# A two-layer decoder trunk: the second half of the features in two parts before each norm, and the last norm on VectorE alone

## The chip, the core and the metric

The kernel runs as one program on one core of a Trainium2 chip. The metric is the device time of one execution in microseconds (us). A core has TensorE (PE in the views; its weight loads are PEld), VectorE (DVE), ScalarE (ACT), GpSimd (POOL) and SyncE (SP), each with its own queue of instructions in program order, and 16 DMA engines. A row that ends in a letter q after the engine's name, as SPq, is an instruction that issues a DMA.

## The reference

The input is 256 rows of 1024 features in float32. There are two layers, and each is

```python
h = layer_norm(ALPHA * h + mix, ln1_g, ln1_b)     # mix: three attention branches, gates, w_out
ffn = (silu(conv3(h @ w_gate) + b) * (h @ w_val)) @ w_down      # D_FF = 2816
h = layer_norm(ALPHA * h + ffn, ln2_g, ln2_b)
# layer_norm(x): (x - mean) * rsqrt(var + 1e-5) * g + b, over the 1024 features of a row
```

The output is h after the second layer, 256 x 1024 float32.

## The kernel before

**Tiles.** The rows are two blocks of 128, `tb` 0 and 1; a block lies on the 128 partitions. `h[tb][q]` is a block's half of the features, 512 columns. Every product is made of three fp32r matmuls (`mm3`: high by high, low by high, high by low); one `mm3` per step k of the contraction is called a unit here. Weights stream from HBM in order of use through `raw` tiles (queue SP) and are split by ScalarE and VectorE into the pairs `hl`.

**The norms.** Four times a norm follows a product: the output projection (first and third norm) and the down projection (second and fourth). Just before each, the last eight units' weights are held ready, and the loop runs `tb`, then `PIECES` (nh, first column, end column), then k: four units for each piece, and then `ln_half`, which on VectorE adds the PSUM bank to ALPHA times h (SCALAR_TENSOR_TENSOR, h<-h,acc) and takes the statistics (BATCH_NORM_STATS2, bst<-h). When both halves of a block are done, `ln_stats` aggregates (mv<-bst), adds epsilon, and lets GpSimd raise to the power -0.5 (rs<-mv,mhalf). `ln_apply` then does, for each half, h<-h,mv,lng (subtract the mean, times g) and h<-h,rs,lnb (times rs, plus b). `ln_tail` transposes each half on TensorE (att<-ident,h, four 128x128 per half) and splits the result into `hTh` (ScalarE) and `hTl` (VectorE, hTl<-att,hTh), the next product's stationary operands. That product takes block 0 first (eight units of 512 columns, k 0 to 3 from the first half of the features, 4 to 7 from the second), then block 1.

**The order.** The program is written out by a planner in Python. Work around the main product lies in generators; `T.tick()`, called after every unit, lets each go on to its next `yield`, and then lets at most one more weight tile be split. A generator yields until its input is due by the planner's own clocks: an instruction starts at its engine's clock or when its inputs are due, and its result is due 150 ns after its end. TensorE takes work only when its clock is 300 ns past that.

```python
rate = {F32: 4, R32: 1, BF16: 1}[args[1].dtype] / 2.4
return n * rate + {F32: 5, R32: 13.3, BF16: 3}[args[1].dtype]   # PE; a transpose is 110
return 60 + n * (0.53 if op in ("tensor_copy", "tensor_scalar") else 1.05)   # DVE
return 75 + 0.85 * n                                            # ACT
return 630 if n <= 16 else 100 + 2.2 * n                        # POOL
while any(clocks.done.get(x.name, 0) > clocks.now(eng) - MARGIN.get(eng, 0) for x in aps):
    yield                                                       # MARGIN = {"PE": 300.0}
```

These clocks order the program; they are no part of its time on the chip. While `W.hold` is set (through a norm) weight tiles are split only when fewer than three are in reserve.

**The last norm.** Behind the fourth norm there is no product. Block 0's is a generator, `last_norm0`: ScalarE normalizes both halves, GpSimd multiplies and adds for the first half, VectorE for the second, which it takes up before block 1's second half. Block 1's is `last_norm1`, on VectorE. Each half is stored as it is done: 128 rows of 2 KB, through the queues of SP and ScalarE.

Of the kernel before, what the change touches and what calls it, by code (L numbers as in the profile page):

```python
# [14 lines left out]
AF = mybir.ActivationFunctionType  # L15
ALU = mybir.AluOpType
AX = mybir.AxisListType

P = 128
# [3 lines left out]
DEPTH = 2  # L23
# [9 lines left out]
           biw=2884, cq=2892, ck=3404, cv=3916)  # L33
NG1 = 332

PIECES = ((0, 0, 512), (1, 0, 512))
MASKED = -1.0e38
PICKED = -3.0e38
PICK_T = -2.0e38
# [248 lines left out]
def tile_hybrid(ctx: ExitStack, tc: tile.TileContext, a: dict, out: bass.AP):  # L288
    nc = tc.nc
    clocks = Clocks()  # L290
    ve, sc = Engine(nc.vector, "DVE", clocks), Engine(nc.scalar, "ACT", clocks)
    pe, gp = Engine(nc.tensor, "PE", clocks), Engine(nc.gpsimd, "POOL", clocks)
# [15 lines left out]
    T = Tasks(clocks, W)  # L308
# [3 lines left out]
    def nm(s):  # L312
        uid[0] += 1
        return f"{s}_{uid[0]}"
# [19 lines left out]
    def small(shape, n="sm"):  # L334
        return ss.tile(shape, F32, name=nm(n), tag="sm")
# [7 lines left out]
    def ready(eng, *aps):  # L343
        while any(clocks.done.get(x.name, 0) > clocks.now(eng) - MARGIN.get(eng, 0) for x in aps):
            yield
# [4 lines left out]
    def mm3(o, lh, ll, rh, rl, start, stop):  # L350
        mm(o, lh, rh, start, False)
        mm(o, ll, rh, False, False)
        mm(o, lh, rl, False, stop)


    h = [[hp.tile([P, 512], F32, name=f"h{t}{q}") for q in range(2)] for t in range(2)]
# [3 lines left out]
    lng = hp.tile([P, D], F32, name="lng0", tag="lng")  # L360
    lnb = hp.tile([P, D], F32, name="lnb0", tag="lnb")
# [106 lines left out]
    def ln_half(tb, q, st, bank=None, cols=(0, 512), slot=None):  # L468

        hs = h[tb][q][:, cols[0]:cols[1]]  # L470
        if bank is not None:
            ve.scalar_tensor_tensor(hs, hs, ALPHA, bank[:, cols[0]:cols[1]], ALU.mult, ALU.add)
        ve.bn_stats(st[:, q if slot is None else slot, :], hs)

    def ln_stats(st):

        mv = small([P, 2], "mv")
        ve.bn_aggr(mv, st)
        ve.tensor_scalar(mv[:, 1:2], mv[:, 1:2], LN_EPS, None, ALU.add)
        rs = small([P, 1], "rs")  # L480
        gp.tensor_tensor(rs, mv[:, 1:2], mhalf[:, :1], ALU.pow)
        return mv[:, 0:1], rs
# [5 lines left out]
            ve.scalar_tensor_tensor(y, y, mu, gq, ALU.subtract, ALU.mult)  # L488
            ve.scalar_tensor_tensor(y, y, rs, bq, ALU.mult, ALU.add)

    def store(tb, q):
        (nc.sync, sc)[q].dma_start(out[0, tb * P:(tb + 1) * P, 512 * q:512 * q + 512], h[tb][q])

    def last_norm1(st, g, b):
        mu, rs = ln_stats(st)
        for q in range(2):
            ve.scalar_tensor_tensor(h[1][q], h[1][q], mu, g[:, 512 * q:512 * q + 512], ALU.subtract, ALU.mult)
        for q in range(2):
            ve.scalar_tensor_tensor(h[1][q], h[1][q], rs, b[:, 512 * q:512 * q + 512], ALU.mult, ALU.add)
            store(1, q)  # L500

    def last_norm0(st, g, b, half_done):

        mu, rs = ln_stats(st)
        nmr = small([P, 1], "nmr")
        ve.scalar_tensor_tensor(nmr, mu, -1.0, rs, ALU.mult, ALU.mult)
        for q in range(2):
            sc.activation(h[0][q], h[0][q], AF.Identity, bias=nmr, scale=rs)
        gp.tensor_tensor(h[0][0], h[0][0], g[:, 0:512], ALU.mult)
        gp.tensor_tensor(h[0][0], h[0][0], b[:, 0:512], ALU.add)  # L510
        while not half_done:
            yield
        ve.tensor_tensor(h[0][1], h[0][1], g[:, 512:1024], ALU.mult)
        ve.tensor_tensor(h[0][1], h[0][1], b[:, 512:1024], ALU.add)
        store(0, 1)
        yield from ready("POOL", h[0][0])
        nc.sync.dma_start(out[0, 0:P, 0:512], h[0][0])

    def transpose4(dst, src, n=4):
        for i in range(n):  # L520
# [6 lines left out]
    def ln_tail(tb, st, hT, g, b, flag):  # L527

        ln_apply(tb, st, g, b)
        yield  # L530
        for q in range(2):
            yield from ready("PE", h[tb][q])
            bk = yield from att()
            transpose4(bk, h[tb][q])
            split_out(hT[0][:, 4 * q:4 * q + 4, tb * P:(tb + 1) * P],
                      hT[1][:, 4 * q:4 * q + 4, tb * P:(tb + 1) * P],
                      bk.rearrange("p (k t) -> p k t", k=4))
            att_free()
        flag.add(tb)
        W.hold = len(flag) < 2  # L540
# [60 lines left out]
    def layer(l, hT, hflag):  # L601
# [384 lines left out]
        lng = hp.tile([P, D], F32, name=nm("lng"), tag="lng")  # L986
        lnb = hp.tile([P, D], F32, name=nm("lnb"), tag="lnb")
# [4 lines left out]
        def gate():  # L992
            bk = unit_x(lhs, KD, 512)
            g = t4([P, 2, 512], n="gs")
            for tb in range(2):
                sc.activation(g[:, tb, :], bk[tb], AF.Sigmoid)
            return g
# [7 lines left out]
        for key in ("oB", "oA"):  # L1005
            for nh in range(2):
                g = gate()
# [46 lines left out]
        hT1, flag1 = new_hT(), set()  # L1054
        for tb in range(2):
            ts = slice(tb * P, (tb + 1) * P)
            st = small([P, 2, 6], "bst")
            for i, (nh, c0, c1) in enumerate(PIECES):
                for k in range(4):
                    w = ws[nh][k][:, :, c0:c1]  # L1060
                    mm3(ob[nh][tb][:, c0:c1], mT[1][:, 0, k, ts], mT[1][:, 1, k, ts], w[:, 0, :], w[:, 1, :],
                        False, k == 3)
                    if tb and c1 == 512:
                        W.free()
                    if True:
                        T.tick()
                ln_half(tb, nh, st, ob[nh][tb], (c0, c1), i)
            T.add(ln_tail(tb, st, hT1, lng, lnb, flag1))
# [29 lines left out]
        lng = hp.tile([P, D], F32, name=nm("lng"), tag="lng")  # L1098
        lnb = hp.tile([P, D], F32, name=nm("lnb"), tag="lnb")
# [61 lines left out]
        hT2, flag2 = new_hT(), set()  # L1161
        for tb in range(2):
            ts = slice(tb * P, (tb + 1) * P)
            st = small([P, 2, 6], "bst")
            for i, (nh, c0, c1) in enumerate(PIECES):
                for d in (NPAIR - 2, NPAIR - 1):
                    T.until(lambda: d in acts)
                    for f in range(2):
                        w = ws[d, f, nh][:, :, c0:c1]
                        mm3(dacc[nh][tb][:, c0:c1], acts[d][:, 0, f, ts], acts[d][:, 1, f, ts],  # L1170
                            w[:, 0, :], w[:, 1, :], False, d == NPAIR - 1 and f == 1)
                        if tb and c1 == 512:
                            W.free()
                        if True:
                            T.tick()
                ln_half(tb, nh, st, dacc[nh][tb], (c0, c1), i)
                if l == DEPTH - 1 and tb and nh == 0:
                    half_done.append(1)
                    T.tick()
            if l < DEPTH - 1:  # L1180
                T.add(ln_tail(tb, st, hT2, lng, lnb, flag2))
            elif tb == 0:
                half_done = []
                T.add(last_norm0(st, lng, lnb, half_done))
            else:
                last_norm1(st, lng, lnb)
        return hT2, flag2


# [29 lines left out]
    for l in range(DEPTH):  # L1219
        hT, hflag = layer(l, hT, hflag)  # L1220
        T.tick()
        while T.live:
            if l < DEPTH - 1 and len(hflag) < 2:
                break
            T.tick()
# [51 lines left out]
```

## Time and profile before

| | us |
|---|---|
| median of 3 runs (lowest, highest) | 935.33 (933.94, 935.53) |
| the profiled execution | 935.33 |
| its span, first to last instruction | 933.5 |
| TensorE busy | 905.1 (97%) |
| VectorE busy | 656.0 (70%) |
| ScalarE busy | 513.5 (55%) |
| GpSimd busy | 47.3 (5%) |

The time of an execution is some 1.8 us longer than its span. Nearly all instructions carry line 240, the line of the helper that records them, so the views are read by tile names: `h<-h,acc` is an instruction that writes h and reads h and acc. In a timeline each line gives the start in us, the busy time in us, the engine, the operation, the tiles, the shapes, how many instructions are merged, and in brackets how long the engine had been idle before and who ended that. PEclk is the clock granted to TensorE as a share of full speed.

### The profile page before, as it was taken

The numbers are of one execution on the slowest core, as the hardware profiler recorded it, in microseconds if no ns is written. First come the engines' busy times: TensorE is split into PE (matmuls) and PEld (weight loads), VectorE is DVE, ScalarE is ACT, GpSimd is POOL, SyncE is SP. The second block draws the span as 40 slices with busy tenths as digits, with TensorE's granted clock in tenths as the row PEclk, the third lists the DMA queues.
The fourth block names the chain that finished last, engine by engine and source line by source line (L and its number), as shares of the span: only waits on it lengthen the run. The fifth ranks groups of instructions, "written<-read, shape, count | busy, mean of one in ns | idle before, by whom it ended". The sixth has DMA issues, their size and how long they took to land.

```text
span 933.5 us, 14405 instructions
## 1 busy us (share of the span) xinstructions
PE 905.1 (97%) x5306; PEld 791.1 (85%) x5306; DVE 656.0 (70%) x1270; ACT 513.5 (55%) x1008; POOL 47.3 (5%) x62
## 2 busy tenths in 40 slices
PE   4999999999999999999999999999999999999995
PEld 2877897888888999999988789888888799999994
DVE  7788677567678766666788966865667886766755
ACT  4654666655536655655456455765554375655541
POOL 6000010001000000000010000100110100000001
PEclk9999999999999999999999999999999999999998
DMA  8843256656535766566345332846665286566601
GB/s 306 275 141 113 69 178 232 188 193 194 181 121 207 245 194 189 172 197 190 113 159 180 123 113 70 298 143 201 192 197 171 87 298 196 181 194 188 182 3 45
DMA packets 46536, 161.45 MB, mean 173 GB/s; under 512 B 5697, under 2 KB 6209, under 8 KB 46465
## 3 DMA queue, kind: packets, MB, share of 16 engines
q1 hardware_dynamic: 44208, 154.94, 51.5%
q0 software_dynamic: 1408, 4.98, 1.7%
q8 instruction: 41, 0.67, 0.3%
q10 hardware_dynamic: 848, 0.60, 0.2%
q14 instruction: 31, 0.25, 0.1%
HBM read 159.46 MB, written 1.05 MB: 172 GB/s over the span
## 4 chain that ended last, share of the span: by engine, by line
PE 70%; issue 21%; DVE 6%; DMA 1%; POOL 1%; ACT 0%; SPq 0%; ACTq 0%; DVEq 0%; POOLq 0%
PE acc L240 49%; PE att L240 21%; DVE h L240 2%; DVE s L240 1%; DMA raw<-in_w_dram 1%; POOL rs L240 1%; DVE hl L240 1%; DMA cst<-in_cst_dram 1%; DVE bst L240 1%; DVE mx L240 0%; DVE mv L240 0%; DVE hTl L240 0%; DVE t L240 0%; ACT h L240 0%; POOL hl L240 0%
## 5 line engine op out<-in xcount | busy, mean ns | idle before, releaser
L240 DVE TENSOR_TENSOR hl<-raw,hl 128x512 fp32r<-128x512 f32 (+1 forms) x581 | 389.5, 696 | 191.3 <-ACT hl L240 189.7
L240 ACT ACTIVATE hl<-raw 128x512 fp32r<-128x512 f32 (+1 forms) x584 | 347.8, 625 | 189.5 <-PE att L240 92.4
L240 PE MATMUL acc<-hl,hTh 128*128 128x512 f32 (+1 forms) x896 | 285.9, 392 | 4.1 <-DVE hl L240 2.0
L240 PE MATMUL att<-hTh,hl 128*128 128x256 f32 x1280 | 231.3, 283 | 0.0
L240 PEld LDWEIGHTS att<-hTh,hl 128*128 128x128 f32 x1280 | 200.8, 192 | 1.4
L240 PEld LDWEIGHTS acc<-hl,hTh 128*128 128x128 f32 x896 | 168.3, 189 | 39.5 <-DVE hl L240 2.7
L240 PE MATMUL att<-hTl,hl 128*128 128x256 f32 x640 | 181.1, 283 | 0.0
L240 PE MATMUL acc<-hl,hTl 128*128 128x512 f32 (+1 forms) x448 | 173.3, 387 | 1.8 <-DVE hTl L240 1.8
L240 PE MATMUL acc<-hl,act 128*128 128x512 f32 x528 | 123.4, 390 | 0.0
L240 PEld LDWEIGHTS att<-hTl,hl 128*128 128x128 f32 x640 | 122.8, 192 | 0.0
L240 PEld LDWEIGHTS acc<-hl,act 128*128 128x128 f32 x528 | 97.9, 188 | 19.5
L240 PEld LDWEIGHTS acc<-hl,hTl 128*128 128x128 f32 x448 | 85.0, 190 | 17.8 <-DVE hTl L240 2.7
L240 PE MATMUL acc<-hl,oT 128*128 128x512 f32 x288 | 68.0, 391 | 0.0
L240 PEld LDWEIGHTS acc<-hl,oT 128*128 128x128 f32 x288 | 53.8, 188 | 11.0
L240 DVE SCALAR_TENSOR_TENSOR cv<-att,convp,cv 128x255 f32<-128x255 f32 x88 | 40.4, 480 | 15.4 <-ACT cv L240 13.9
L240 PE MATMUL acc<-hTh,hl 128*128 128x256 f32 x256 | 47.7, 287 | 0.0
L240 PE MATMUL acc<-hl,mT 128*128 128x512 f32 x192 | 45.4, 392 | 0.0
L240 ACT ACTIVATE hTh<-att 128x512 fp32r<-128x512 f32 x16 | 9.6, 598 | 59.2 <-PE att L240 59.1
L240 PEld LDWEIGHTS acc<-hl,mT 128*128 128x128 f32 x192 | 35.6, 188 | 7.1
L240 PEld LDWEIGHTS acc<-hTh,hl 128*128 128x128 f32 x256 | 39.8, 191 | 2.0 <-issue 1.7
L240 PE MATMUL acc<-hTl,hl 128*128 128x256 f32 x128 | 36.2, 283 | 0.0
L240 POOL TENSOR_TENSOR rs<-mv,mhalf 128x1 f32<-128x1 f32 x10 | 9.1, 906 | 482.4 <-DVE mv L240 482.4
(160 smaller groups left out, 696.6 us busy)
## 6 DMA issues: line engine op xcount, KB each, us to landing
raw<-in_w_dram SPq DMA_DIRECT2D x284, 512.0 KB, 4.2
raw<-in_w_dram SPq DMA_DIRECT2D x8, 332.0 KB, 4.4
lng<-in_ln_g_dram POOLq DMA_DIRECT2D x4, 512.0 KB, 4.0
lnb<-in_ln_b_dram POOLq DMA_DIRECT2D x4, 512.0 KB, 5.9
h<-in_x_dram SPq DMA_DIRECT2D x4, 256.0 KB, 4.9
lng<-in_ln_in_g_dram SPq DMA_DIRECT2D x2, 256.0 KB, 5.2
lnb<-in_ln_in_b_dram SPq DMA_DIRECT2D x2, 256.0 KB, 5.2
wu<-in_w_ukv_dram POOLq DMA_DIRECT2D x2, 256.0 KB, 3.0
```

Of the source, the lines that this page charges most:

```text
L240: f(*args, **kw)
```

## The change

`PIECES` has three entries: the first half of the features as before, the second half as columns 0 to 255 and 256 to 511 of its bank. This holds for all four norms; each part has its matmuls, its addition and its statistics, and the aggregate reads 18 numbers per row instead of 12. `last_norm0` and `last_norm1` give way to one `last_norm`, all on VectorE, run directly where the block's statistics end, with stores of 512, 256 and 256 columns through SP, ScalarE and SP.

```diff
-PIECES = ((0, 0, 512), (1, 0, 512))
+PIECES = ((0, 0, 512), (1, 0, 256), (1, 256, 512))
...
-    def store(tb, q):
-        (nc.sync, sc)[q].dma_start(out[0, tb * P:(tb + 1) * P, 512 * q:512 * q + 512], h[tb][q])
-
-    def last_norm1(st, g, b):
+    def last_norm(tb, st, g, b):
         mu, rs = ln_stats(st)
         for q in range(2):
-            ve.scalar_tensor_tensor(h[1][q], h[1][q], mu, g[:, 512 * q:512 * q + 512], ALU.subtract, ALU.mult)
-        for q in range(2):
-            ve.scalar_tensor_tensor(h[1][q], h[1][q], rs, b[:, 512 * q:512 * q + 512], ALU.mult, ALU.add)
-            store(1, q)
-
-    def last_norm0(st, g, b, half_done):
-
-        mu, rs = ln_stats(st)
-        nmr = small([P, 1], "nmr")
-        ve.scalar_tensor_tensor(nmr, mu, -1.0, rs, ALU.mult, ALU.mult)
-        for q in range(2):
-            sc.activation(h[0][q], h[0][q], AF.Identity, bias=nmr, scale=rs)
-        gp.tensor_tensor(h[0][0], h[0][0], g[:, 0:512], ALU.mult)
-        gp.tensor_tensor(h[0][0], h[0][0], b[:, 0:512], ALU.add)
-        while not half_done:
-            yield
-        ve.tensor_tensor(h[0][1], h[0][1], g[:, 512:1024], ALU.mult)
-        ve.tensor_tensor(h[0][1], h[0][1], b[:, 512:1024], ALU.add)
-        store(0, 1)
-        yield from ready("POOL", h[0][0])
-        nc.sync.dma_start(out[0, 0:P, 0:512], h[0][0])
+            ve.scalar_tensor_tensor(h[tb][q], h[tb][q], mu, g[:, 512 * q:512 * q + 512], ALU.subtract, ALU.mult)
+        for i, (c0, c1) in enumerate(((0, 512), (512, 768), (768, 1024))):
+            y = h[tb][c0 // 512][:, c0 % 512:c0 % 512 + c1 - c0]
+            ve.scalar_tensor_tensor(y, y, rs, b[:, c0:c1], ALU.mult, ALU.add)
+            (nc.sync, sc, nc.sync)[i].dma_start(out[0, tb * P:(tb + 1) * P, c0:c1], y)
...
-            st = small([P, 2, 6], "bst")
+            st = small([P, 3, 6], "bst")
...
                 ln_half(tb, nh, st, dacc[nh][tb], (c0, c1), i)
-                if l == DEPTH - 1 and tb and nh == 0:
-                    half_done.append(1)
-                    T.tick()
             if l < DEPTH - 1:
                 T.add(ln_tail(tb, st, hT2, lng, lnb, flag2))
-            elif tb == 0:
-                half_done = []
-                T.add(last_norm0(st, lng, lnb, half_done))
             else:
-                last_norm1(st, lng, lnb)
+                last_norm(tb, st, lng, lnb)
```

## Rows read from the trace of the kernel before

**Rows 1.** Stretches (us): length, busy time by engine (instructions), PEclk, DMA share, GB/s.

```profile
278.00:282.00 4.00, 3.40 (x20) 2.53 (x19) 3.93 (x7) 1.50 (x3) 0.00 (x0) 1.00 0.02 4
...
296.00:456.00 160.00, 160.00 (x1156) 152.00 (x1155) 108.48 (x180) 94.42 (x161) 0.00 (x0) 1.00 0.62 198
```

**Rows 2.** Timeline of the first norm, VectorE and TensorE.

```profile
274.75 0.69 DVE L240 SCALAR_TENSOR_TENSOR h<-h,acc 128x512 f32<-128x512 f32 x1 [1.30 <-PE acc L240]
...
279.83 0.68 DVE L240 SCALAR_TENSOR_TENSOR h<-h,acc 128x512 f32<-128x512 f32 x1
...
281.16 1.27 DVE L240 TENSOR_TENSOR hTl<-att,hTh 128x512 fp32r<-128x512 f32 x2
...
281.89 0.50 PE L240 MATMUL acc<-hl,hTl 128*128 128x512 f32 x1 [0.60 <-DVE hTl L240]
...
282.35 0.68 DVE L240 SCALAR_TENSOR_TENSOR h<-h,acc 128x512 f32<-128x512 f32 x1
...
283.79 0.21 DVE L240 BATCH_NORM_AGGREGATE mv<-bst 128x2 f32<-128x12 f32 x1
...
286.20 0.63 PE L240 MATMUL att<-ident,h 128*128 128x128 f32 x4
...
286.58 0.47 PE L240 MATMUL acc<-hl,hTh 128*128 128x512 f32 x1
...
287.65 0.63 PE L240 MATMUL att<-ident,h 128*128 128x128 f32 x4
...
288.03 0.48 PE L240 MATMUL acc<-hl,hTh 128*128 128x512 f32 x1
```

**Rows 3.** Timeline of TensorE, matmuls of 256 columns, every third.

```profile
903.20 0.28 PE L240 MATMUL att<-hTl,hl 128*128 128x256 f32 x1
...
903.56 0.28 PE L240 MATMUL att<-hTl,hl 128*128 128x256 f32 x1
```

**Rows 4.** Timeline of the last norm: VectorE, and the issues of stores.

```profile
915.67 0.69 DVE L240 SCALAR_TENSOR_TENSOR h<-h,acc 128x512 f32<-128x512 f32 x1 [3.10 <-PE acc L240]
...
918.39 0.69 DVE L240 SCALAR_TENSOR_TENSOR h<-h,acc 128x512 f32<-128x512 f32 x1 [1.30 <-PE acc L240]
...
925.44 0.68 DVE L240 SCALAR_TENSOR_TENSOR h<-h,acc 128x512 f32<-128x512 f32 x1
...
925.55 4.75 ACTq L240 DMA_DIRECT2D out_dram<-h  x2
...
926.88 0.21 DVE L240 BATCH_NORM_AGGREGATE mv<-bst 128x2 f32<-128x12 f32 x1
...
927.19 1.40 DVE L240 SCALAR_TENSOR_TENSOR h<-h,mv,lng 128x512 f32<-128x512 f32 x2
...
928.51 1.41 DVE L240 SCALAR_TENSOR_TENSOR h<-h,rs,lnb 128x512 f32<-128x512 f32 x2
...
929.28 0.35 SPq L492 DMA_DIRECT2D out_dram<-h  x1
...
929.73 0.38 SPq L517 DMA_DIRECT2D out_dram<-h  x1
```

**Rows 5.** VectorE's groups by line and form: narrower instructions.

```profile
L240 DVE MAX8 mx<-s 128x8 f32<-128x256 f32 x16 | 6.5, 409 | 0.0
...
L240 DVE SCALAR_TENSOR_TENSOR t<-t,rr,kvg 128x256 f32<-128x256 f32 x4 | 1.8, 484 | 0.0
```

**Rows 6.** DMA issues of the last stretch: count, KB each, median us to landing.

```profile
out_dram<-h SPq DMA_DIRECT2D x2, 256.0 KB, 2.1
...
out_dram<-h ACTq DMA_DIRECT2D x1, 256.0 KB, 2.6
```

**Rows 7.** TensorE's timeline at two idle times; the stretch behind the first.

```profile
22.60 0.80 PE L240 MATMUL acc<-hl,hTh 128*128 128x512 f32 x1 [1.97 <-DVE hl L240]
...
74.41 1.06 PE L240 MATMUL att<-ident,t 128*128 128x128 f32 x8 [1.41 <-DVE t L240]
...
22.00:27.00 5.00, 4.40 (x15) 3.62 (x16) 4.20 (x11) 2.72 (x8) 1.29 (x6) 0.66 0.77 205
```

More of the change, by code (lines that the diff above doesn't have):

```diff
@@ L1163, in layer @@
             ts = slice(tb * P, (tb + 1) * P)
-            st = small([P, 2, 6], "bst")
+            st = small([P, 3, 6], "bst")
             for i, (nh, c0, c1) in enumerate(PIECES):
```

## Prediction

> **What bounds the kernel now.** I read the busy times in stretches first, to see where TensorE stands still. Through the 160 us of the first gated MLP it is busy all the time [rows 1]; around each of the first three norms it stands still a little, 0.60 in the stretch that is shown [rows 1], and its clock stays at the upper level, 2.4 GHz. So TensorE sets the time up to the last norm, the three inner norms are places where VectorE gets in its way, and behind the last matmul VectorE and the stores set the end. The second and the third norm repeat the first's pattern, so the first is shown.
>
> Second, the timeline of the first norm [rows 2]. VectorE adds and aggregates block 0 from 274.75, then works without a gap that matters: block 1's first half at 279.83, both hTl, block 1's second half at 282.35 although TensorE had finished it earlier, the aggregate at 283.79. TensorE waits 0.60 for hTl at 281.89, and the transposes of block 1 at 286.20 and 287.65 start right when VectorE has written h. What TensorE gets back, it loses again to this VectorE chain, unless the chain itself becomes shorter.
>
> Third, the last norm [rows 4]: block 0's second half is added at 918.39, block 1's second half only at 925.44, because block 0's norm occupies VectorE in between; the last write of h ends at 928.51 + 1.41 = 929.92. ScalarE's second store is issued at 925.55 + 4.75 - 0.35 = 929.95 (an issue takes about as long as SP's 0.35) and lands 2.6 later [rows 6], at 932.55; 0.95 later the span ends.
>
> **What a part of 256 columns costs.** For TensorE: three matmuls of 256 take 903.56 - 903.20 = 0.36 [rows 3], twelve of 512 take 918.39 - 915.67 = 2.72 [rows 4]. The second half is 24 x 0.12 = 2.88 instead of 2.72: 0.16 more per block. For VectorE: two dependent instructions of 512 take 283.79 - 282.35 = 1.44 [rows 2], 0.72 each. A scalar_tensor_tensor of 256 columns with a pointer scalar takes 0.484 [rows 5]; of 512, from the pair at 927.19 (1.40 in all, the next pair 1.32 later, so 0.66 apart), 0.74 [rows 4]. The narrow one saves d = 0.26, and costs 0.46 where the next waits for it, 0.40 where not. BATCH_NORM_STATS2 of 256 columns does not occur. The nearest is MAX8, also one input and statistics out, 0.409 at 256 [rows 5], against 0.69 of instructions of 512 [rows 2]; its bounds are a saving of nothing and of one half, 0.36. I take 0.26, as for its neighbour.
>
> The row says that 256 columns cost 0.484. [...]
>
> **An inner norm.** Block 0's second half ends 0.16 later on TensorE, but only the last quarter's two instructions follow: 0.92 instead of 1.44. The aggregate comes 0.36 earlier, and so block 1's first half: 279.83 - 0.36 = 279.47. Then VectorE, in the program's order: that half's two instructions, 281.16 - 279.83 = 1.33; hTl, 0.60 (half of 282.35 - 281.16); block 1's first quarter-part, 0.46 + 0.35; hTl, 0.60; the second part, 0.92: the aggregate at 283.73. Before: 283.79. Splitting block 1 costs nearly all that splitting block 0 gives. In d: the change is 1.49 - 6d, -0.07.
>
> TensorE's order moves too. I worked the planner's clocks by hand (costs as quoted above; a unit is 0.68, of 256 columns 0.36, four transposes 0.44). For the kernel before, counted from the end of block 0, they make block 1's first transposes due at 11.48, behind six units of the next product (11.73), and the second due at 12.82, behind seven (12.85); the trace has this order. With three parts, the first are due at 10.81, behind five units (10.93), the second at 12.16, still behind seven (12.73). TensorE executes in order: the 0.60 for hTl goes, it begins the next product at about 274.75 + 0.16 + 2.72 + 2.88 + 2 x 0.38 = 281.27, runs up to the transposes one unit early, by 284.7 (five units), and stands there until h is written, 286.20 - 0.07 = 286.13: some 1.4 us. Then transposes 0.38 (286.58 - 286.20), two units 1.36 instead of one, transposes 0.38: the eighth unit starts at 288.25, before at 288.03 [rows 2]. Each inner norm costs 0.22 more, three cost **+0.66**. Nothing hides this, since TensorE is full behind it [rows 1]. Behind the standing transposes wait two units, and on ScalarE the splits of the next weights behind hTh; three splits in reserve cover those. The extra ticks bring no additional weight splits, because the reserve is held through the norm.
>
> **The last norm.** There is no product behind it, so VectorE's queue alone counts. The last part of block 0 is ready at 918.39 + 0.16 = 918.55; 0.92; aggregate and epsilon 927.19 - 926.88 = 0.31; two subtractions 1.32 (GpSimd's power runs beneath them, as it does at 927.19); three additions of b 0.66 + 0.40 + 0.40: 922.56. ScalarE's two passes, GpSimd's two and VectorE's own two tensor_tensors for block 0 are gone. Block 1, ready since 921.27: first half 1.33, first part 0.81: 924.70, where the last part is ready too (918.55 + 2.72 + 2.88 = 924.15); 0.92, 0.31, 1.32: the additions of b start at 927.25. The last ends 0.66 + 0.40 + 0.48 later, at 928.79 instead of 929.92: -1.13 (in d: 1.47 - 10d).
>
> The stores: block 0's three go out near 922 to 923, beneath block 1's work; SP's and ScalarE's queues hold nothing else by then but the later stores. The last, of 128 KB on SP, is issued at 928.82. SP's stores of 256 KB landed after 2.1, ScalarE's, queued behind those two [rows 4], after 2.6 [rows 6]. For half the bytes I take 1.8, nearest to SP's row; the bounds are half of 2.1 and 2.6. Landing at 930.62, plus 0.95: 931.57 instead of 933.5, **-1.93**. The stores alone are -0.8 of it.
>
> **The sum.** -1.93 + 0.66 = -1.27. On the profiled execution (935.33, its span 933.5 and 1.8 around it; the median of the runs is the same number) that is **934.1**.
>
> **The rivals.** About 0.2%, 1.9 us, is what a measurement of this kernel can tell from no change.
>
> *Faster.* If TensorE does not run into the early transposes, or the inner norms otherwise come out at the -0.07 of the VectorE chain, the sum is -1.93 - 0.2 = -2.1: 933.2. If statistics cost one half, d there is 0.36, and 12 such instructions (three in each norm) give another -1.2: 932.9. For it: the forecast lies only 0.6 from the mark. Against it: two instructions that wait for nothing still show 0.40 apart for 256 columns.
>
> *The cut saves nothing in the statistics.* With d = 0 for the 12 statistics the sum is -1.27 + 3.12 = +1.85: 937.2, just at the mark. MAX8 speaks against it.
>
> *Slower: the stall lowers the clock.* The stall of 1.4 us that I expect at each inner norm is new. At 22.60, after 1.97 of idle time, TensorE went on at half clock: over five microseconds the mean is 0.66 [rows 7], so 0.34 x 5 = 1.7 us lost. At three norms that is 5.1: 935.33 - 1.27 + 5.1 = 939.2; from two norms on (+2.1) it decides the sign. Against it: after an idle time of 1.41 the matmuls went on at full clock, the transposes at 74.41 taking 1.06 for eight [rows 7]. [...]
>
> *The stores land no sooner.* With 2.6 for the last: 934.9, still no change that can be told.
>
> **Chances.** No change that can be told, my forecast with its neighbours: 0.58. Faster 0.34, by the first rival or by the sum of small errors. Clock 0.05, statistics 0.03, most of these slower: 0.08 together. The likeliest is 934.1; its own bounds are 932.8 to 936.0: d from 0.22 (the pair's 1.40 read as 0.70 each) to 0.28 (MAX8) in 28 instructions, 18 at the inner norms and 10 at the last, is +1.1 to -0.6, the landing +0.8 to -0.75. The range for 8 in 10 reaches to the faster rival and past the forecast's upper bound: 932.2 to 936.0.
>
> **What would show it.** In the new profile: additions and statistics of 128x256 near 0.43 each; no wait for hTl at the first norm, but a wait of more than 1 us before the transposes of block 1, which come after five units of the next product and after seven; the eighth unit 0.2 later than before; VectorE without gaps from 918.5 to the end; the last store about 1.1 earlier and the span's end about 1.9 earlier after the last matmul. It is wrong if TensorE stands less at the transposes, if PEclk falls below 1.00 at a norm, or if the 256-column matmuls take more than 0.12 each.

## The result, and the profile after

The change made the kernel slower: 946.5 us (944.82 to 947.9, 4 runs) against 935.43 for the kernel before in the same comparison, a ratio of 1.012 (95% interval 1.0107 to 1.0132). The forecast was 934.1, in a range of 932.2 to 936.0. The profiled execution took 946.39, its span is 944.6, and the mean granted clock 0.992 (before 0.995).

The first view to read is that of TensorE's waits. Its columns are: who waits for whom, us in total, how often, the longest.

```profile
PE acc L240 <- DVE h L240: 10.6, 8, 2.3
...
PE att L240 <- DVE h L240: 0.3, 1, 0.3
```

The first line does not exist before. TensorE, about to write `acc`, waits eight times for VectorE to have written `h`: twice in each of the four norms. The wait for hTl, which the kernel before has in this view as

```profile
PE acc L240 <- DVE hTl L240: 1.8, 3, 0.6
```

is gone, and the forecast wait of the transposes for h (second line above) hardly exists. The timeline of the first norm, VectorE and TensorE, shows what the new wait is:

```profile
273.40 0.42 DVE L240 SCALAR_TENSOR_TENSOR h<-h,acc 128x256 f32<-128x256 f32 x1
...
273.88 5.15 PE L240 MATMUL acc<-hl,mT 128*128 128x256 f32 x30 [0.51 <-DVE h L240]
...
276.52 0.23 DVE L240 BATCH_NORM_AGGREGATE mv<-bst 128x2 f32<-128x18 f32 x1
...
280.19 0.68 DVE L240 SCALAR_TENSOR_TENSOR h<-h,acc 128x512 f32<-128x512 f32 x1
...
281.51 0.67 DVE L240 TENSOR_TENSOR hTl<-att,hTh 128x512 fp32r<-128x512 f32 x1
282.11 0.41 DVE L240 SCALAR_TENSOR_TENSOR h<-h,acc 128x256 f32<-128x256 f32 x1
...
282.57 0.62 PE L240 MATMUL acc<-hl,mT 128*128 128x256 f32 x3 [2.26 <-DVE h L240]
...
283.38 1.31 PE L240 MATMUL acc<-hl,mT 128*128 128x256 f32 x9
...
284.90 0.41 DVE L240 SCALAR_TENSOR_TENSOR h<-h,acc 128x256 f32<-128x256 f32 x1
...
288.25 0.63 PE L240 MATMUL att<-ident,h 128*128 128x128 f32 x4
...
289.70 0.63 PE L240 MATMUL att<-ident,h 128*128 128x128 f32 x4
```

Both of TensorE's waits end some 0.05 after an addition of 256 columns: 273.40 + 0.42 = 273.82 and 273.88; 282.11 + 0.41 = 282.52 and 282.57. Those additions read columns 0 to 255 of a bank of `acc`, and the matmuls that wait write columns 256 to 511 of the same bank. In block 0 VectorE is free and the wait is 0.51. In block 1 VectorE must first finish block 0's norm (from the aggregate at 276.52), add block 1's first half (280.19) and write hTl; only then does it come to the addition at 282.11, and TensorE stands for 2.26. Compare [rows 2], where TensorE had finished block 1's second half before VectorE came to it at 282.35.

The other norms repeat this: 0.51 and 2.33 at the second, 0.51 and 2.26 at the third. The stretches of 2 us behind the long wait show a second loss. The columns are length, busy time of PE, PEld, DVE, ACT and POOL (instructions), PEclk, DMA share, GB/s.

```profile
280.00:282.00 2.00, 0.31 (x3) 0.10 (x1) 1.97 (x4) 0.23 (x1) 0.00 (x0) 1.00 0.00 0
282.00:284.00 2.00, 1.43 (x12) 1.43 (x13) 0.94 (x3) 0.34 (x1) 0.00 (x0) 1.00 0.00 0
...
476.00:478.00 2.00, 2.00 (x12) 2.00 (x12) 0.20 (x2) 0.69 (x2) 0.00 (x0) 0.53 0.00 0
478.00:480.00 2.00, 2.00 (x10) 1.81 (x10) 1.37 (x3) 1.19 (x1) 0.00 (x0) 0.61 0.00 0
...
742.00:744.00 2.00, 1.79 (x9) 1.79 (x10) 0.58 (x2) 0.02 (x1) 0.00 (x0) 0.59 0.00 0
744.00:746.00 2.00, 2.00 (x11) 1.95 (x11) 0.79 (x2) 0.58 (x1) 0.00 (x0) 0.55 0.00 0
```

At the first norm PEclk stays at 1.00 behind the idle time of 2.26; at the second (2.33) it is 0.53 and 0.61 in the two stretches behind it, at the third (2.26) 0.59 and 0.55. The last norm, VectorE and TensorE, to be read beside [rows 4]:

```profile
926.13 0.69 DVE L240 SCALAR_TENSOR_TENSOR h<-h,acc 128x512 f32<-128x512 f32 x1 [3.10 <-PE acc L240]
...
928.04 5.88 PE L240 MATMUL acc<-hl,act 128*128 128x256 f32 x36 [0.52 <-DVE h L240]
...
935.14 0.40 DVE L240 SCALAR_TENSOR_TENSOR h<-h,acc 128x256 f32<-128x256 f32 x1
...
935.60 1.69 PE L240 MATMUL acc<-hl,act 128*128 128x256 f32 x12 [1.68 <-DVE h L240]
937.32 0.42 DVE L240 SCALAR_TENSOR_TENSOR h<-h,acc 128x256 f32<-128x256 f32 x1 [1.32 <-PE acc L240]
...
938.58 1.40 DVE L240 SCALAR_TENSOR_TENSOR h<-h,mv,lng 128x512 f32<-128x512 f32 x2
...
939.90 1.53 DVE L240 SCALAR_TENSOR_TENSOR h<-h,rs,lnb 128x512 f32<-128x512 f32 x3
```

The same two waits, 0.52 and 1.68, and behind the second one it is VectorE that stands (1.32 before 937.32).

Where the time went is read from the first h<-h,acc of each norm, since where the first one lies differs by up to 1.5 us between the traces:

| | before | after | difference |
|---|---|---|---|
| first to second norm | 190.37 | 193.15 | +2.78 |
| second to third | 262.92 | 266.49 | +3.57 |
| third to last | 190.36 | 194.52 | +4.16 |
| last norm to the span's end | 17.83 | 18.47 | +0.64 |

The three inner norms cost 10.51, forecast 0.66; the last norm +0.64, forecast -1.93.

### The profile page after: what moved, and what is told of

It is laid out like the page before. It is cut to its first block, busy times and chain, and to the rows that moved or that the text cites. A ratio compares the mean times of both kernels' runs of the same rounds, so it can differ in the third digit from the quotient of the medians.

```text
span 944.6 us, 14612 instructions
## 1 busy us (share of the span) xinstructions
PE 910.3 (96%) x5402; PEld 800.0 (85%) x5402; DVE 659.5 (70%) x1289; ACT 512.0 (54%) x1006; POOL 44.6 (5%) x60
## 5 line engine op out<-in xcount | busy, mean ns | idle before, releaser
L240 PE MATMUL acc<-hl,act 128*128 128x512 f32 (+1 forms) x576 | 126.3, 375 | 5.0 <-DVE h L240 5.0
L240 PEld LDWEIGHTS acc<-hl,act 128*128 128x128 f32 x576 | 102.0, 191 | 23.8 <-DVE h L240 5.8
L240 PE MATMUL acc<-hl,mT 128*128 128x512 f32 (+1 forms) x240 | 48.7, 358 | 5.5 <-DVE h L240 5.5
L240 PEld LDWEIGHTS acc<-hl,mT 128*128 128x128 f32 x240 | 40.0, 195 | 11.9 <-DVE h L240 6.4
```

What stands on the lines that cost most here:

```text
L240: f(*args, **kw)
```

## The theories and the experiments

**The bank theory.** TensorE's matmuls into one part of a PSUM bank (here one `acc` or `att` tile, 512 columns in which TensorE sums up a product) wait until VectorE has read the other part of that bank. What sets the time is then when VectorE comes to that addition, above all in block 1.

**The rivals.** (1) Narrow matmuls or narrow VectorE instructions cost more than the forecast had. (2) The last norm, moved to VectorE, is what is slow. (3) The fall of the clock is the loss, and the wait by itself little. Each run below is a ratio to the kernel before, measured on the same chip in the same comparison (935.41, 935.46 and 935.1 us in the three).

### Each half of the change alone

The first kernel keeps two whole halves before each norm and takes only the new last norm; the second takes only the three parts, and keeps the old last norm.

```diff
 PIECES = ((0, 0, 512), (1, 0, 512))        # first kernel; st stays [P, 2, 6]
-                last_norm1(st, lng, lnb)
+                last_norm(tb, st, lng, lnb)
```

> The last norm is changed alone; the halves stay whole at all four norms. Bank theory (TensorE may not write the second part of a PSUM bank until VectorE has read the first): no part, no wait, so the new last norm keeps its gain. VectorE: 919.84 + 0.31 + 1.32 + 1.46 = 922.9, block 1 by 2.8 and then 0.31 + 1.32 + 1.54, so b ends at about 928.9 instead of 929.92, and with the smaller last store the span ends about 1.8 earlier: 933.5. Rival (the last norm on VectorE alone is itself the loss, or a part of it): 936 or more.

```diff
-PIECES = ((0, 0, 512), (1, 0, 512))        # second kernel; last_norm0 and last_norm1 stay
+PIECES = ((0, 0, 512), (1, 0, 256), (1, 256, 512))
```

> The three pieces alone, with the last norm as before. Bank theory: the three inner norms cost what they cost in the changed kernel, 10.5, and the last norm waits for banks too: 946 to 948. Rival (the last norm is the loss): near 936.

The last norm alone: 933.89 us (932.99 to 934.65), ratio 0.9985 (0.9976 to 0.9994). From its first addition to the span's end it takes 16.40 instead of 17.83, and the distances between the norms are those of before within 0.04. The parts alone: 948.09 (947.47 to 949.13, a little over the 946 to 948 expected), ratio 1.014 (1.0125 to 1.0155), with eight waits of TensorE for h, 11.8 in all. Rival 2 falls: the last norm gains 1.4, and all of the loss comes with the parts.

### The cut on one engine alone

In one kernel only TensorE's matmuls are cut; VectorE adds and takes statistics of the whole second half behind both parts. In the other the matmuls stay whole and only VectorE's work is cut in two. Both have the new last norm.

```diff
-                ln_half(tb, nh, st, ob[nh][tb], (c0, c1), i)
+                if c1 == 512:                      # matmuls cut
+                    ln_half(tb, nh, st, ob[nh][tb], (0, 512), nh)
```

> The changed kernel, but VectorE adds and takes statistics of the second half in one, after both of its parts' matmuls. Bank theory: VectorE never reads a bank that TensorE still writes, so the waits go: 24 matmuls of 256 cost 0.16 more per block, 0.3 to 0.5 per inner norm, and the last norm keeps its gain: 934.5 to 935.5. Rival (narrow matmuls, or the other order of the program that comes with twelve ticks instead of eight, are the loss): 942 or more.

```diff
+PIECES = ((0, 0, 512), (1, 0, 512))                # VectorE cut
...
+                    ln_half(tb, nh, st, ob[nh][tb], (0, 256), 1)
+                    ln_half(tb, nh, st, ob[nh][tb], (256, 512), 2)
```

> Matmuls whole as before, but VectorE adds and takes statistics of the second half in two parts of 256 after them; last norm as in the changed kernel. Bank theory: nothing to wait for; only two more VectorE instructions per block, 0.46 + 0.35 + 0.46 + 0.46 = 1.73 instead of 1.44, so some 0.6 per inner norm and 0.6 at the last, on the 933.9 of the last norm alone: 936. Rival (VectorE's narrow instructions are the loss): 942 or more.

Matmuls cut: 934.49 (933.28 to 935.1), ratio 0.9993 (0.9984 to 1.0003). The distances between the norms are 190.52, 263.05 and 190.53: some 0.15 more than before for 48 narrow matmuls instead of 24 wide ones (net: the waits for hTl shrink from 1.8 to 0.8 in all); no wait of TensorE for an addition into the same bank. VectorE cut: 936.98 (935.47 to 937.37), ratio 1.0015 (1.0006 to 1.0024). That is 1 us over what was expected. Its longer chain makes TensorE wait longer for hTl, where [rows 2] had 0.60, and then for a weight tile (`hl`) that VectorE splits only behind the norm, as in TensorE's timeline of the first norm:

```profile
282.38 0.50 PE L240 MATMUL acc<-hl,hTl 128*128 128x512 f32 x1 [0.89 <-DVE hTl L240]
...
288.92 0.50 PE L240 MATMUL acc<-hl,hTh 128*128 128x512 f32 x1 [0.76 <-DVE hl L240]
```

The second wait is there at all three inner norms (0.76, 0.82, 0.81) and at none before. Beside the new last norm alone (ratio 0.9985) the two cuts add 0.0008 and 0.0030, the change 0.0135: neither cut by itself costs a quarter of what both together do. Rival 1 falls as the main cause.

### The third part in a bank of its own

The whole change, but the third part's matmuls write an `att` bank that nothing else uses, and VectorE adds it in an instruction more. (The old bank still holds what earlier units summed up in columns 256 to 511, so the addition at the second part goes over all 512.)

```diff
+                own = get_bank() if i == 2 else None
...
-                    mm3(ob[nh][tb][:, c0:c1], ...
+                    mm3(own[:, 0:256] if i == 2 else ob[nh][tb][:, c0:c1], ...
...
+            ve.tensor_tensor(h[tb][1][:, 256:512], h[tb][1][:, 256:512], extra[:, 0:256], ALU.add)
```

> The changed kernel, but the third part's last matmuls go to a PSUM bank of their own, and VectorE adds that bank in addition; with the second part it adds the whole old bank, so two instructions of 256 become one of 512 and one of 256. Bank theory: no wait of TensorE for h at the third part, no clock drop; the forecast's sum holds but for 0.3 more VectorE time per block: 934.5 to 936. Rival (the cut costs by its instructions, its order or its statistics, whichever the bank): as the changed kernel, 945 to 948.

Measured: 936.48 (935.15 to 936.81), half a microsecond over what was expected, ratio 1.0012 (1.0002 to 1.0022). Ten of the eleven microseconds are gone with the shared bank, and the granted clock is 0.998 in the mean. What is left is the stall that the prediction had expected, in TensorE's timeline:

```profile
285.65 0.66 PE L240 MATMUL att<-ident,h 128*128 128x128 f32 x4 [1.26 <-DVE h L240]
```

It is 1.26 long, forecast 1.4, and the norms cost +0.87, +0.50 and +0.86 (191.24, 263.42 and 191.22 between them), forecast +0.22 each. Of the 0.65 by which the first is over the forecast, 0.27 to 0.54 would be this kernel's own: in each block VectorE adds 512 columns (0.684) where the change adds 256 (0.418). That is an estimate from those two durations.

### Which block pays

Three parts for block 0 alone, and for block 1 alone; the rest as in the change.

```diff
-PIECES = ((0, 0, 512), (1, 0, 256), (1, 256, 512))
+PIECES = (((0, 0, 512), (1, 0, 256), (1, 256, 512)), ((0, 0, 512), (1, 0, 512)))    # block 0 alone
...
+            for i, (nh, c0, c1) in enumerate(PIECES[tb]):
```

> The cut in three pieces only for block 0; block 1 in halves. Bank theory: at block 0 VectorE is free and reads the second part's bank at once, so the wait is the 0.5 of one addition, and the 2.3 at block 1 is gone, with it the fall of the clock: PEclk 1.00 at all norms. The aggregate of block 0 comes 0.4 later than before: 1.2 for three norms and 0.4 at the last on 933.9: 935.5. Rival (the loss is shared evenly by the two blocks' cuts): about 940.

> Three pieces (512, 256, 256 columns) for token block 1 alone; block 0 keeps two halves. If TensorE's third piece waits for VectorE's addition of the second piece out of the same PSUM bank, block 1 keeps its wait of about 2.3 us per inner norm (longer if VectorE is still at block 0's norm), block 0 has none, and the granted clock falls behind that wait at some norms: 943 to 945 us, 942.7 if the clock does not fall. If the loss is shared evenly by the two blocks whatever VectorE is doing, about half of it is left: 940 us.

Block 0 alone: 935.26 (933.72 to 936.23), ratio 0.9995 (0.9986 to 1.0004), with four waits of 0.5. Block 1 alone: 945.35 (944.53 to 947.08), ratio 1.0119 (1.0102 to 1.0136). The waits of the two, of TensorE for an addition, first block 0 alone:

```profile
PE acc L240 <- DVE h L240: 2.1, 4, 0.5
```

and block 1 alone:

```profile
PE acc L240 <- DVE h L240: 11.0, 4, 2.9
```

Block 1's waits are four instead of eight, and their total is no less: without block 0's 0.5, TensorE is at block 1's third part sooner and waits 2.9 there instead of 2.3. The end of the wait is set by VectorE, not by how many waits come before it. The time is 0.35 over the upper end of what was expected.

### Keeping TensorE busy through the wait

In front of block 1's third part, at the three inner norms, seven matmuls of 512 columns go into a spare bank; nothing reads them. The wait for VectorE stays as it is, and TensorE is not idle through most of it.

```diff
+                if tb and i == 2:
+                    keep_busy(mT[1][:, 0, 0, ts], ws[1][3][:, 0, :])    # 7 matmuls into a spare bank
```

> The changed kernel; in front of block 1's third piece at the three inner norms, where TensorE waits 2.3 for VectorE, seven matmuls of 512 columns (1.6) into a spare bank whose result nobody reads. If the fall of the clock behind the wait is a cost of its own, PEclk stays at 1.00 at the second and third norm and the kernel is about 2.0 faster than the changed one: 944.5. If the clock is only a sign and the time between the norms is lost elsewhere, 946.5 stays.

Measured: 944.32 (942.76 to 944.88), ratio 1.0091 (1.0077 to 1.0105). TensorE's timeline of the second norm:

```profile
472.16 1.77 PE L488 MATMUL att<-hl,act 128*128 128x512 f32 x7
474.65 0.62 PE L240 MATMUL acc<-hl,act 128*128 128x256 f32 x3 [0.72 <-DVE h L240]
```

The stretches behind the wait, at the second and the third norm, where the change had 0.53 and 0.59:

```profile
476.00:478.00 2.00, 2.00 (x13) 1.75 (x12) 1.56 (x4) 1.62 (x2) 0.00 (x0) 1.00 0.00 0
...
742.00:744.00 2.00, 2.00 (x11) 1.62 (x10) 1.90 (x6) 0.00 (x0) 0.31 (x1) 1.00 0.00 0
```

PEclk is 1.00 at all three norms, and the distances are 193.17, 265.29 and 193.17 (the change 193.15, 266.49 and 194.52). The first, where the clock had not fallen, is the same; the other two are 1.20 and 1.35 shorter. So the clock costs 2.55 of the 10.51, and rival 3 falls: with the clock up all the time, 8.9 us remain.

### Parts taken from the two banks in turn

If the bank is the cause, the order of the parts should decide. Here block 0's four quarters come from the two banks alternately, so that a whole quarter lies between two parts of one bank; block 1 keeps its halves. In the second kernel both blocks alternate.

```diff
-PIECES = ((0, 0, 512), (1, 0, 256), (1, 256, 512))
+PIECES = (((0, 0, 256), (1, 0, 256), (0, 256, 512), (1, 256, 512)), ((0, 0, 512), (1, 0, 512)))
```

> Block 0 in four pieces of 256, taken alternately from its two banks; block 1 in halves. Bank theory: VectorE reads one bank while TensorE writes the other, a piece's 1.44 is longer than an addition's 0.46, so no wait at all; the last piece leaves 0.92 instead of 1.44 on VectorE, TensorE pays 0.32: the aggregate 0.2 earlier, three norms -0.6 and the last -0.2 on 933.9: 933.1. Rival (any cut costs): 936 or more.

> Both token blocks in quarters of 256 columns taken alternately from the two PSUM banks. If the wait is for the addition of the last piece of the same bank, block 0 has no wait, as its pieces have a whole piece of the other bank between them, but block 1's third piece waits about 1.8 us for the addition of its first, since VectorE is at block 0's norm until then: some 1.3 to 1.5 us per inner norm and 1 us at the last over the kernel with alternation for block 0 alone (933.05 us): 938 to 939 us, with the granted clock at full speed. If alternation takes away every wait: 934 us or less.

Block 0 alternating: 933.05 (931.31 to 933.97), ratio 0.9969 (0.996 to 0.9979), the fastest kernel here, and below the kernel before. (The new last norm alone has 0.9985; the two intervals just overlap, so they do not settle that the alternation itself gains, though the distances are shorter too: 190.20, 262.32, 190.20.) VectorE's additions at its first norm come every 1.44, twelve matmuls of 0.12, so TensorE runs through:

```profile
271.57 0.42 DVE L240 SCALAR_TENSOR_TENSOR h<-h,acc 128x256 f32<-128x256 f32 x1 [1.44 <-PE acc L240]
...
273.01 0.42 DVE L240 SCALAR_TENSOR_TENSOR h<-h,acc 128x256 f32<-128x256 f32 x1 [0.56 <-PE acc L240]
...
274.45 0.42 DVE L240 SCALAR_TENSOR_TENSOR h<-h,acc 128x256 f32<-128x256 f32 x1 [0.56 <-PE acc L240]
```

Both blocks alternating: 944.31 (943.17 to 945.9), ratio 1.0106 (1.0091 to 1.0121). The place was forecast rightly, the size not. Block 0 has no wait, and block 1's third part waits for the addition of its first:

```profile
279.78 0.42 DVE L240 SCALAR_TENSOR_TENSOR h<-h,acc 128x256 f32<-128x256 f32 x1
...
280.25 0.98 PE L240 MATMUL acc<-hl,mT 128*128 128x256 f32 x6 [2.25 <-DVE h L240]
```

It waits 2.25, where I had expected 1.8, and nothing gives any of it back, where I had netted it to 1.5. Against block 0 alternating the norms cost +2.52, +3.80 and +3.80; the two 1.28 more are again those where the clock falls, which I had not counted. So alternating banks takes the wait away here only where VectorE drains as fast as TensorE fills: in block 0 its addition and its statistics take 0.42 + 0.43 of each 1.44. In block 1 VectorE is at block 0's norm, and what avoids the wait is bank space, as in the kernel before: two whole banks, each filled before VectorE comes to it (279.83 and 282.35 [rows 2]).

## Why the prediction was wrong

**The step that failed** is the pair "For TensorE: ... The second half is 24 x 0.12 = 2.88 instead of 2.72: 0.16 more per block" and, in the inner norm, the run of TensorE to "about 274.75 + 0.16 + 2.72 + 2.88 + 2 x 0.38 = 281.27". Both priced the matmuls and none of them priced a wait inside the cut bank. The durations are right (1.44 for twelve), but between the two twelves of one bank stands VectorE's addition: 0.51 in block 0, 2.26 to 2.33 in block 1. With the third part in a bank of its own, nearly the same program comes to 936.48, half a microsecond above the range.

The rows of before told how long such a wait would be: TensorE fills block 1's second half while VectorE is still at block 0's norm, and VectorE's addition comes only at 282.35 [rows 2]. A wait for an addition in the middle of that half has to end there. That there would be such a wait none of those rows shows; the runs do. It ends 0.05 after the addition (273.82 and 273.88, 282.52 and 282.57), though the columns are not the same. With parts from the two banks in turn TensorE does not wait in block 0 (933.05); in both blocks (944.31) it waits 2.25 in block 1, where the reader is late. A bank is here one `acc` or `att` tile, and in every run two parts share both or neither, so no run tells a wait for the bank from a wait for the tile, and whether the hardware would have needed the wait at these columns was not tried.

**Point by point.**

- VectorE's narrow instructions: right. The groups by line and form (busy us, mean ns):

```profile
L240 DVE BATCH_NORM_STATS2 bst<-h 128x6 f32<-128x256 f32 x16 | 6.8, 428 | 0.6
L240 DVE SCALAR_TENSOR_TENSOR h<-h,acc 128x256 f32<-128x256 f32 x16 | 6.7, 418 | 7.9 <-PE acc L240 7.8
```

  against 0.69 and 0.68 for 512 columns: d is 0.26, as taken, for statistics too, and the rival that statistics save nothing is out.
- "The 0.60 for hTl goes": it does, but because TensorE now arrives later, not because VectorE is sooner.
- The planner's order: the first transposes of block 1 come behind five units, as forecast; the second behind six, not seven. Their stall of 1.4 does not show in the change, as the bank's wait has used it up; it shows at 1.26 as soon as that wait is away.
- The last norm: -1.93 forecast. Alone it gives -1.43 with whole halves. In the change it is +0.64: from the first addition to the last it takes 937.32 - 926.13 = 11.19 instead of the forecast 924.70 - 915.67 = 9.03, and the two waits, 0.52 + 1.68 = 2.20, account for the 2.16 between them; from there to the span's end 7.28 instead of 6.87. Stores of 128 KB on SP land after 1.9, forecast 1.8.
- The clock as a rival: right that a new stall can lower it (PEclk 0.53 behind the 2.33 of the second norm, 0.59 behind the 2.26 of the third); wrong in the place of the stall and in the price, 1.20 and 1.35 instead of 1.7. (The fall itself is as large as forecast: at the second norm 0.47 x 2 + 0.39 x 2 = 1.72; not all of it became time.) The upper level, PEclk 1.00, which the prediction gives as 2.4 GHz, is 2.4 columns in a ns by its own rows: 256 columns more take 2.72 / 12 - 0.36 / 3 = 0.107 [rows 3, rows 4].

**The sum by what was measured,** for the three inner norms: six waits for the bank 8.38, the three waits for hTl no longer there -1.8, the narrow matmuls 3 x 0.32 = 0.96, the clock 2.55, in all 10.09 of 10.51. The remaining 0.4 was not traced. With +0.64 at the last norm, and 0.05 by which the first norm lay earlier, this is the 11.1 by which the spans differ (944.6 and 933.5).

## What to carry to other kernels

When an accumulation is to be drained sooner in smaller parts, cut it along PSUM banks, not within one (here 936.48 and 946.5): a part of the same bank waited here until the reader had finished the part before it, and the reader's queue at that time, not the length of its instruction, set the price (0.5 us with VectorE free, 1.7 to 2.9 with a norm in front). Before pricing a finer cut, look in the timeline for when the reader gets to that bank now; where it comes late, as at 282.35 in [rows 2], the bank is a buffer that the cut takes away. Take parts from two banks in turn where the reader keeps up (here, in block 0, that took the wait away; a gain over whole halves is not settled), and leave them whole where it does not (here block 1: 933.05 with whole halves, 944.31 in turn).

## What the runs showed of the hardware

In these runs the clock's fall behind an idle time is not decided by its length alone. In four kernels each of three inner norms has an idle time of 2.2 to 2.9 us (the change, the parts alone, block 1 alone, both blocks alternating); in eight of these twelve the clock fell (PEclk 0.50 to 0.72 in the lowest stretch of 2 or 4 us at that norm), in the other four it stayed at 1.00. With block 1 alone the wait is 2.9 at all three (2.92, 2.91, 2.92), and behind the first and the third the stretches read:

```profile
284.00:286.00 2.00, 2.00 (x11) 1.90 (x10) 0.87 (x2) 0.60 (x1) 0.00 (x0) 0.50 0.00 0
...
744.00:746.00 2.00, 2.00 (x12) 1.67 (x11) 1.68 (x4) 0.19 (x1) 0.00 (x0) 1.00 0.00 0
```

At the first PEclk is 0.50, at the third 1.00, as in the stretches of 2 us before and behind that one. So the same wait, 2.92, in one execution ended with either clock; what decides it was not shown, and at which waits the clock would fall could not be told ahead.

The price of a fall differs as well, 1.35 and 0.70 here. The distances behind the first and the third norm can be compared, as the same work follows; the one behind the second has other work and is cheaper also where no clock falls (+2.37 beside +2.80 and +2.81 with TensorE kept busy). The change loses 1.35 at its third norm by the fall. Block 1 alone loses +3.42 at the first norm, where the clock falls, and +2.72 at the third, where it stays up: 0.70. There TensorE, with the clock up, stands again before the transposes of block 1:

```profile
748.17 0.63 PE L240 MATMUL att<-ident,h 128*128 128x128 f32 x4 [0.47 <-DVE h L240]
```

With the clock down, at the first norm, it comes there later and has no such wait (289.45, no idle time before), so part of that fall lies under a wait of 0.47 that comes without it.
